# Sums of squares with fewer one-column matmuls, and reciprocal row sums brought to 64 partitions through DRAM instead of by transposes

## The chip, the cores and the metric

The kernel runs on one core of one Trainium2 chip. The metric is the device time of one execution in microseconds; smaller is better. The core has five engines that run in parallel, each working off its own queue in order: TensorE (PE, with its weight loads as PEld), VectorE (DVE), ScalarE (ACT), GpSimd (POOL) and SyncE (SP). Here every DMA is issued from SP's queue. Matmuls and transposes write PSUM; DVE and ACT read PSUM and SBUF, POOL reads SBUF only.

## What is computed

Two layers of a decoder trunk on 1024 tokens of width 1024, in f32. The parts that matter here:

```
qa, ka, va -> y_a : window attention, 6 heads of 64
y_b : latent attention, causal, 6 heads of 64:
    p = softmax(scores);  y_b[q, h, :] = sum_k p[q, k] v[k, h, :]
y_c : gated chunks
y = concat(rms_norm(y_a, gw_a), rms_norm(y_b, gw_b), rms_norm(y_c, gw_c))
x = x + g1 * (y @ w_out)
... then a SwiGLU block, and after both layers a final rms_norm
```

`rms_norm` divides by the root of the mean of squares over a group's columns: 384 for y_a and for y_b. The softmax's division by the row sum is made after the product with v.

## The kernel before, in words

Tokens are cut into 8 tiles of 128 and into two halves of 512 (Q = 0, 1). Matmuls are made in three passes over a high and a low part of each operand (`mm3`, lines 134 to 136), so that most matrices are split by ACT (the high part) and DVE (the low part, line 139).

Each layer has these stages. **Stage A**: input projections and window attention, with the latent projections. **Stage B**: latent attention, 12 groups (head, half), first the six heads of half 1 and then those of half 0. **Tail of B**: the output projection's tiles are mixed in with the last groups. Then normalisation, the SwiGLU block in two large stages, all matmul.

Within a stage the work is a set of generators, and a string written out by hand (`PRU0`, `PRU1` for A; `PRB0`, `PRB1` for B) says which takes its next step. A scheduler then puts each engine's instructions in a fixed order at compile time, near the program's, where an instruction that is not ready may be passed by a later one.

**y_a (stage A).** `a_av` writes a tile's window-attention output in transposed form, 3 chunks of 128 columns, for 128 tokens. ACT squares it (line 940). `group_rstd` sums the squares over the 384 columns with matmuls whose moving operand is one column of ones: three for a tile, added up in PSUM (line 540). DVE copies the sums out (542), and POOL's `rstd` makes the power -1/2 (171, 172). An f32 matmul is two passes in the trace.

**y_b (stage B).** Per group: `head_prep` transposes q and k; `b_soft` makes scores and exponentials of 4 tiles with their row sums in `sm`, [128, 4]; `b_av` has two generators. `gen_t` takes the reciprocals of `sm` (line 1197) and transposes the probabilities to `pTs`, unit by unit. `gen_m` multiplies with v, and its end `fin` makes the output: four transposes (line 1221) bring the reciprocals, broadcast along 64 columns, to 64 partitions in a PSUM bank `rT`; ACT and DVE add the two halves of the product (1223, 1225), and DVE multiplies by `rT` into `y32` (1226). After every two heads of a half `sq_pair` squares the 128x512 chunk (ACT, line 949), sums it with four one-column matmuls (953), copies the four columns out (955) and adds them to the last sum on POOL (957); after the third it calls `rstd`.

**The output projection.** `w_out`'s columns 0 to 511 were prepared earlier and are loaded as `wo`. Columns 512 to 1023 are loaded in `load_wout` as eight 128x512 tiles `wor` (line 1239), multiplied on POOL by the gate row `mrow` (line 1090), and split by ACT (146) and DVE (147) into `woh` and `wol`. `out_tile` uses them for the tiles of its second column half. `load_x` (1252) loads residual tiles as buffers of the tag "g" come free.

**Buffers.** A tag has a fixed number of buffers. "ad" has 4 of 128x512 f32 (`AD`): `qk` and `lowk` in stage A, `wor` in the tail of B, others later. "s" has 4 (`SM`): `sqB`, `tmpB` and more. PSUM in B has 4 single banks (`PA`: `pTB`, `qkTB`, `avB`, `rT`, `sq`) and 2 double ones (`PB`: scores).

Of the kernel before, what the change touches and what calls it, by code (L numbers as in the profile page):

```python
# [8 lines left out]
F32 = mybir.dt.float32  # L9
F32R = mybir.dt.float32r  # L10
I32 = mybir.dt.int32
AF = mybir.ActivationFunctionType
ALU = mybir.AluOpType
AX = mybir.AxisListType

P = 128
# [4 lines left out]
DEPTH = 2  # L21
# [57 lines left out]
def tile_trunk(ctx, tc, x, c, positions, ada_w, ada_b, norm1_w, w_in, a_sinks, b_q_norm_w, b_w_uq,  # L79
# [3 lines left out]
    ACT, DVE, POOL, PE, DMA = nc.scalar, nc.vector, nc.gpsimd, nc.tensor, nc.sync  # L83
# [5 lines left out]
    dr = ctx.enter_context(tc.tile_pool(name="dr", bufs=1, space=bass.MemoryType.DRAM))  # L89
    uid = [0]  # L90

    def nm(s):
        uid[0] += 1
        return f"{s}_{uid[0]}"
# [13 lines left out]
    def G(shape, dt=F32, name="g"):  # L108
        return gp.tile(shape, dt, tag="g", name=nm(name), bufs=NG)
# [7 lines left out]
    def SM(shape, dt=F32, name="s"):  # L117
        return sp.tile(shape, dt, tag="s", name=nm(name))

    def TN(w=8, name="t"):  # L120
        t = tp.tile([P, 8], F32, tag="t", name=nm(name))
        return t[:, :w]

    def PA(name="pa"):
        return ps_pool["a"].tile([P, 512], F32, tag="a", name=nm(name))
# [23 lines left out]
    def AD(name="ad", shape=(P, 512), dt=F32):  # L149
        return sp.tile(list(shape), dt, tag="ad", name=nm(name), bufs=NAD)  # L150

    def chunk(ap, k):
        return ap[:, k * P:(k + 1) * P]

    psum_banks(8, 0)
    ident = cst.tile([P, P], F32, name="ident")
    make_identity(nc, ident)
    ones = cst.tile([P, P], F32, name="ones")
# [10 lines left out]
    def rstd(dst, ss, n, w=1):  # L169
        v = TN(w, "ms")  # L170
        POOL.tensor_scalar(out=v, in0=ss, scalar1=1.0 / n, scalar2=EPS, op0=ALU.mult, op1=ALU.add)  # L171
        POOL.tensor_tensor(out=dst, in0=v, in1=mhalf[:, :w], op=ALU.pow)  # L172
# [180 lines left out]
    def rope(q, nh, half, t, f0):  # L353
# [20 lines left out]
    wpd = [{j: [dr.tile([P, 2, 512], F32, name=f"wp{l}_{j}_{i}") for i in range(7)] for j in EARLY[l]}  # L374
           for l in range(DEPTH)]
    cqd = [[dr.tile([P, 384], F32, name=f"cq{l}_{t}") for t in range(NT)] for l in range(DEPTH)]
    yad = [[dr.tile([P, 3, 512], F32, name=f"ya{l}_{hf}") for hf in range(2)] for l in range(DEPTH)]

    def ada_finish(l, j, mc, wait=1):
# [155 lines left out]
    def group_rstd(sq, n, dst):  # L535

        ps = PA("sq")
        for i in range(n):
            for k in range(3):
                PE.matmul(ps[:, i:i + 1], sq(k, i), ones[:, 0:1], start=(k == 0), stop=(k == 2))  # L540
        r = TN(n, "sc")
        DVE.tensor_copy(out=r, in_=ps[:, :n])
        rstd(dst, r, 384, n)

    def layer(l, x_tiles):
# [6 lines left out]
        rs_a = cst.tile([P, 8], F32, name=f"rsa{l}")  # L552
        rs_b = cst.tile([P, 8], F32, name=f"rsb{l}")
# [57 lines left out]
        y32 = [[None, None] for _ in range(4)]  # L611
# [38 lines left out]
        if l == 0:  # L650
# [39 lines left out]
            def l_seq():  # L690
                for kp in range(4):
                    if kp >= 2:
                        need("a", 8)
                    raw_w.append(load_w1(kp, acc0[0]))
                    yield

            def s_seq():
                for kp in range(4):
                    need("l", kp + 1)
                    split_w1(raw_w[kp], POOL if SP0[kp] else DVE)  # L700
                    yield

            def h_seq():
                need("s", 2)
                for t in range(NE):
                    need("m", t + 1)
                    avq[t] = PA("avq")
                    in_proj(avq[t], T[t], w1, 0, 4)
                    yield
# [30 lines left out]
            def g_seq():  # L740
# [6 lines left out]
                                    l=l_seq(), s=s_seq(), h=h_seq(), v=v_seq(), C=c_seq(), G=g_seq(), B=bg_seq()))  # L747
# [6 lines left out]
        else:  # L754
# [4 lines left out]
            for i, t in enumerate(ordA):  # L759
# [6 lines left out]
                ps = PA("avq")  # L766
# [19 lines left out]
        qk, qs_t, ks_t, qva, kwin, prs_a, y_a = {}, {}, {}, {}, {}, {}, {}  # L786
# [132 lines left out]
        def a_av(t, g):  # L919
            ph, pl = prs_a.pop((t, g))  # L920
            js = (1,) if t == 0 else (0, 1)
            po = PA("avA")
            for j in js:
                v = qva[t - 1 + j][:, 6 + g, :]
                PE.matmul(po[:, :384], v, ph[:, j, :], start=(j == js[0]), stop=False)
                PE.matmul(po[:, :384], v, pl[:, j, :], start=False, stop=(j == 1))
            tmp = SM([64, 384], F32, "tmpA")
            ACT.copy(out=tmp, in_=po[64:128, :384])
            if g == 0:
                y_a[t] = G([P, 2, 3, P], F32, "yA")  # L930
            for i in range(3):
                h = 3 * g + i
                k, r0 = h // 2, (h % 2) * 64
                DVE.tensor_tensor(out=y_a[t][r0:r0 + 64, 0, k, :], in0=chunk(po[0:64, :], i), in1=chunk(tmp, i),
                                  op=ALU.add)
            if g == 1:
                y = y_a.pop(t)
                hf, tt = t // 4, t % 4
                DMA.dma_start(out=yad[l][hf][:, :, tt * P:(tt + 1) * P], in_=y[:, 0])
                ACT.activation(out=y[:, 1], in_=y[:, 0], func=AF.Square)  # L940
                return lambda: group_rstd(lambda k, i: y[:, 1, k, :], 1, rs_a[:, t:t + 1])

        sqs = {}

        def sq_pair(p, Q):

            k = 3 + p
            sq = SM([P, 512], F32, "sqB")
            ACT.activation(out=sq, in_=y32[k // 2][Q][:, k % 2, :], func=AF.Square)
            yield  # L950
            ps = PA("sq")
            for i in range(4):
                PE.matmul(ps[:, i:i + 1], chunk(sq, i), ones[:, 0:1], start=True, stop=True)
            r = sqs[p, Q] = TN(4, "sc")
            DVE.tensor_copy(out=r, in_=ps[:, :4])
            if p > 0:
                POOL.tensor_tensor(out=r, in0=r, in1=sqs[p - 1, Q], op=ALU.add)
            if p == 2:
                rstd(rs_b[:, 4 * Q:4 * Q + 4], r, 384, 4)

# [210 lines left out]
        def b_av(h, Q, prs, sm):  # L1173

            d = 4 * Q
            units = [(j,) for j in range(d + 1)] + [(d + 1, d + 3), (d + 2,)]

            def tr(u):
                pt_ = PA("pTB")
                o = max(0, u[0] - d) * P if len(u) == 1 else 0  # L1180
                spans = []
                for j in u:
                    a = max(0, j - d)
                    s0 = 0 if j != u[0] else a * P
                    for i in range(a, 4):
                        c = s0 + (i - a) * P
                        PE.transpose(pt_[:, c:c + P], prs[i][:, j * P:(j + 1) * P], ident)
                    spans.append((j, a * P, slice(s0, s0 + (4 - a) * P)))
                pt2 = R([P, 2, 512], F32R, "pTs")
                ACT.copy(out=pt2[:, 0, o:], in_=pt_[:, o:])  # L1190
                sub(DVE, pt2[:, 1, o:], pt_[:, o:], f32(pt2[:, 0, o:]))
                return spans, pt2

            ready = []

            def gen_t():
                DVE.reciprocal(out=sm, in_=sm)
                for u in units:
                    ready.append(tr(u))
                    yield  # L1200

            def gen_m():
                po = PA("avB")
                for n in range(len(units)):
                    if n >= len(ready):
                        step("T")
                    spans, pt2 = ready[n]
                    last = n + 1 == len(units)
                    for j, o, cs in spans:
                        v = vB[j][:, h].rearrange("p a e -> p (a e)")  # L1210
                        PE.matmul(po[:, o:], v, pt2[:, 0, cs], start=(n == 0), stop=False)
                        PE.matmul(po[:, o:], v, pt2[:, 1, cs], start=False, stop=last)
                    yield
                fin(po)
                done.append(h)
                yield

            def fin(po):
                pr_ = PA("rT")
                for i in range(4):  # L1220
                    PE.transpose(pr_[:64, i * P:(i + 1) * P], sm[:, i:i + 1].to_broadcast([P, 64]), ident)
                tmp = SM([64, 512], F32, "tmpB")
                ACT.copy(out=tmp, in_=po[64:128, :])
                k, r0 = 3 + h // 2, (h % 2) * 64
                DVE.tensor_tensor(out=tmp, in0=po[0:64, :], in1=tmp, op=ALU.add)
                DVE.tensor_tensor(out=y32[k // 2][Q][r0:r0 + 64, k % 2, :], in0=pr_[:64, :], in1=tmp, op=ALU.mult)

            return gen_t(), gen_m()

# [381 lines left out]
        ready = []  # L1611
# [74 lines left out]
        def pair_seq():  # L1686
# [5 lines left out]
                    t=build_t_seq(), j=load_gu_seq(), r=prep_gu_seq(), s=pair_seq())  # L1692
# [71 lines left out]
```

## Time and profile before

| | |
|---|---|
| time, median of 3 runs | 2386.37 us (2384.11 to 2387.43) |
| the profiled execution | 2389.68 us, span 2387.7 us |
| mean granted TensorE clock | 0.979 |
| PE busy, share of the span | 2261.8 us, 95% |
| DVE | 1792.9 us, 75% |
| ACT | 1100.3 us, 46% |
| POOL | 1024.3 us, 43% |
| DMA, mean over the span | 146 GB/s |

How to read the profile: busy time is the time in which an engine has an instruction under way. Matmuls overlap, since the next starts while the last drains, so the time that one holds PE is read from the start of one to the start of the next. A group row gives the count, then the busy time in us and the mean in ns of one instruction, then the idle time of its engine just before it and what ended that. Rows in order of time give start and length in us. A wait row gives who waited for whom: total us, times, longest. Stage A is at about 130 to 330 us in layer 0 and 1300 to 1500 in layer 1, B with its tail at 339 to 469 and 1526 to 1656.

### The profile page before, as it was taken

To read this page: it belongs to the slowest core of one execution; us is meant where nothing else is said; L and a number is where in the kernel's file an instruction comes from. 1 tells how busy PE (TensorE), PEld (TensorE's weight loads), DVE (VectorE), ACT (ScalarE), POOL (GpSimd) and SP (SyncE) were. 2 spreads that over 40 slices of the span, in tenths; PEclk is the share of its full clock that TensorE was granted. 3 is DMA by queue.
4 is the path that set the end of the run, shared out by engine and by line. 5 is a ranking of instruction groups with operands and counts; after the bars stand their busy time and mean duration, and the time that the engine had idled before them with its cause. 6 is when DMAs were issued, how large, how long until landed. Compare 5 with 4: busy or idle time off the path is not lost. (4 is left out here: it accounts for less than half of the span.)

```text
span 2387.7 us, 31998 instructions
## 1 busy us (share of the span) xinstructions
PE 2261.8 (95%) x11195; PEld 1906.9 (80%) x11195; DVE 1792.9 (75%) x2787; ACT 1100.3 (46%) x2244; POOL 1024.3 (43%) x1011
## 2 busy tenths in 40 slices
PE   5999899998999999999999989899989999999998
PEld 4789798887887788778878878788877888887786
DVE  7787578859787776699974765788598767648978
ACT  4566377625333444223344654685354444433233
POOL 4755630343332433545554656212435334225643
PEclk9999999999999999999999999999999999999999
DMA  7403432312577654862241044323125545467433
GB/s 254 164 19 117 166 130 89 115 45 93 177 248 241 211 188 160 316 234 90 80 156 40 24 130 168 111 80 115 54 77 192 194 153 182 164 217 286 158 106 115
DMA packets 156036, 349.77 MB, mean 146 GB/s; under 512 B 12618, under 2 KB 71780, under 8 KB 155876
## 3 DMA queue, kind: packets, MB, share of 16 engines
q1 hardware_dynamic: 155876, 347.74, 42.3%
q8 instruction: 88, 1.44, 0.3%
q14 instruction: 72, 0.59, 0.1%
HBM read 252.75 MB, written 94.94 MB: 146 GB/s over the span
## 5 line engine op out<-in xcount | busy, mean ns | idle before, releaser
L139 DVE TENSOR_TENSOR gus<-gur,gus 128x512 fp32r<-128x512 f32 x264 | 255.5, 985 | 59.9 <-ACT gus L142 59.0
L142 ACT CAST gus<-gur 128x512 fp32r<-128x512 f32 x264 | 160.9, 621 | 219.2 <-PE gate L136 85.0
L134 PE MATMUL down<-dnt,dns 128*128 128x512 f32 x616 | 241.8, 393 | 13.2 <-ACT dnt L142 6.8
L134 PE MATMUL gate<-hTh,gus 128*128 128x512 f32 x616 | 242.8, 394 | 11.8 <-ACT u L1505 10.4
L135 PE MATMUL gate<-hTl,gus 128*128 128x512 f32 x616 | 241.4, 392 | 4.4 <-DVE hTl L139 4.4
L134 PE MATMUL up<-hTh,gus 128*128 128x512 f32 x616 | 241.0, 391 | 1.5 <-ACT u L1510 1.5
L135 PE MATMUL down<-dnt,dns 128*128 128x512 f32 x616 | 241.2, 391 | 0.0
L136 PE MATMUL down<-dnt,dns 128*128 128x512 f32 x616 | 240.8, 391 | 0.0
L136 PE MATMUL gate<-hTh,gus 128*128 128x512 f32 x616 | 240.8, 391 | 0.0
L135 PE MATMUL up<-hTl,gus 128*128 128x512 f32 x616 | 240.6, 391 | 0.0
L136 PE MATMUL up<-hTh,gus 128*128 128x512 f32 x616 | 240.4, 390 | 0.0
L1417 POOL TENSOR_TENSOR gur<-gur 128x512 f32<-128x512 f32 x44 | 67.2, 1528 | 389.6 <-DVE gus L139 389.6
L142 ACT CAST dns<-act 128x512 fp32r<-128x512 f32 x132 | 81.8, 622 | 250.3 <-PE down L136 189.6
L1595 DVE TENSOR_TENSOR x<-x,down 128x512 f32<-128x512 f32 x224 | 148.1, 679 | 31.5 <-PE down L136 31.2
L134 PEld LDWEIGHTS down<-dnt,dns 128*128 128x128 f32 x616 | 116.4, 189 | 41.2 <-issue 6.0
L134 PEld LDWEIGHTS gate<-hTh,gus 128*128 128x128 f32 x616 | 116.4, 189 | 39.1 <-ACT u L1505 12.3
L139 DVE TENSOR_TENSOR dns<-act,dns 128x512 fp32r<-128x512 f32 x132 | 136.3, 1048 | 12.9 <-ACT dns L142 12.9
L135 PEld LDWEIGHTS gate<-hTl,gus 128*128 128x128 f32 x616 | 116.4, 189 | 29.5 <-DVE hTl L139 6.0
L134 PEld LDWEIGHTS up<-hTh,gus 128*128 128x128 f32 x616 | 116.4, 189 | 26.1 <-ACT u L1510 2.0
L136 PEld LDWEIGHTS down<-dnt,dns 128*128 128x128 f32 x616 | 116.5, 189 | 24.3
L136 PEld LDWEIGHTS gate<-hTh,gus 128*128 128x128 f32 x616 | 116.4, 189 | 24.4
L135 PEld LDWEIGHTS up<-hTl,gus 128*128 128x128 f32 x616 | 116.3, 189 | 24.1
(410 smaller groups left out, 6165.1 us busy)
## 6 DMA issues: line engine op xcount, KB each, us to landing
gur<-in_w_gate_up_dram SPq DMA_DIRECT2D x88, 512.0 KB
ada<-in_ada_w_dram SPq DMA_DIRECT2D x80, 512.0 KB
wp<-wpe SPq DMA_DIRECT2D x77, 512.0 KB
dnt<-wp SPq DMA_DIRECT2D x77, 512.0 KB
dnr<-in_w_down_dram SPq DMA_DIRECT2D x44, 512.0 KB
act<-act SPq DMA_DIRECT2D x44, 512.0 KB
wr<-in_w_in_dram SPq DMA_DIRECT2D x24, 512.0 KB
act<-u SPq DMA_DIRECT2D x44, 256.0 KB
```

Source lines behind the costliest of these rows:

```text
L134: PE.matmul(ps, lh, rh, start=start, stop=False, skip_group_check=more)
L135: PE.matmul(ps, lh, rl, start=False, stop=False, skip_group_check=more)
L136: PE.matmul(ps, ll, rh, start=False, stop=stop, skip_group_check=more)
L139: eng.tensor_tensor(out=out_, in0=a, in1=b, op=ALU.subtract)
L142: ACT.copy(out=h, in_=src)
L1417: return lambda o, a, b, op: eng.tensor_tensor(out=o, in0=a, in1=b, op=op)
L1595: DVE.tensor_tensor(out=av_, in0=av_, in1=ps[t], op=ALU.add)
```

## The change

Four edits.

1. `a_av` squares into chunks 3 to 5 of one tile, and POOL adds the second and third chunk's squares to the first's (two 128x128 adds for each of 16 tiles). `group_rstd` takes the sum, so there is one one-column matmul for a tile instead of three.
2. `sq_pair` keeps the first pair's squares in an `AD` buffer; DVE adds the second's and third's squares to it (128x512), and the one-column matmuls are made once for a half, in `group_rstd`, instead of after every two heads. The three copies and two small POOL adds become one copy.
3. `gen_t` stores the reciprocals right after they are made: `sm`, [128, 4], goes to a DRAM tile of 4 rows of 128, in pieces of one element; a second DMA loads the 512 values as one row onto each of 64 partitions, into an `AD` buffer `rB`.
4. `fin` multiplies by `rB` instead of `rT`; the four transposes and their PSUM bank go.

```diff
+    rsd = [[[dr.tile([4, P], F32, name=f"rs{l}_{h}_{hf}") for hf in range(2)] for h in range(6)] for l in range(DEPTH)]
...
         for i in range(n):
-            for k in range(3):
-                PE.matmul(ps[:, i:i + 1], sq(k, i), ones[:, 0:1], start=(k == 0), stop=(k == 2))
+            PE.matmul(ps[:, i:i + 1], chunk(sq, i), ones[:, 0:1], start=True, stop=True)
...
-                DMA.dma_start(out=yad[l][hf][:, :, tt * P:(tt + 1) * P], in_=y[:, 0])
-                ACT.activation(out=y[:, 1], in_=y[:, 0], func=AF.Square)
-                return lambda: group_rstd(lambda k, i: y[:, 1, k, :], 1, rs_a[:, t:t + 1])
+                DMA.dma_start(out=yad[l][hf][:, :, tt * P:(tt + 1) * P], in_=y[:, 0:3])
+                ACT.activation(out=y[:, 3:6], in_=y[:, 0:3], func=AF.Square)
+                for k in (4, 5):
+                    POOL.tensor_tensor(out=y[:, 3, :], in0=y[:, 3, :], in1=y[:, k, :], op=ALU.add)
+                return lambda: group_rstd(y[:, 3, :], 1, rs_a[:, t:t + 1])
...
-            sq = SM([P, 512], F32, "sqB")
+            sq = AD("sqB") if p == 0 else SM([P, 512], F32, "sqB")
             ACT.activation(out=sq, in_=y32[k // 2][Q][:, k % 2, :], func=AF.Square)
             yield
-            ps = PA("sq")
-            for i in range(4):
-                PE.matmul(ps[:, i:i + 1], chunk(sq, i), ones[:, 0:1], start=True, stop=True)
-            r = sqs[p, Q] = TN(4, "sc")
-            DVE.tensor_copy(out=r, in_=ps[:, :4])
-            if p > 0:
-                POOL.tensor_tensor(out=r, in0=r, in1=sqs[p - 1, Q], op=ALU.add)
+            if p == 0:
+                sqs[Q] = sq
+            else:
+                DVE.tensor_tensor(out=sqs[Q], in0=sqs[Q], in1=sq, op=ALU.add)
             if p == 2:
-                rstd(rs_b[:, 4 * Q:4 * Q + 4], r, 384, 4)
+                group_rstd(sqs[Q], 4, rs_b[:, 4 * Q:4 * Q + 4])
...
-            ready = []
+            ready, rb = [], []
 
             def gen_t():
                 DVE.reciprocal(out=sm, in_=sm)
+                DMA.dma_start(out=rsd[l][h][Q].rearrange("i p -> p i"), in_=sm)
+                rb.append(AD("rB", [64, 512]))
+                DMA.dma_start(out=rb[0], in_=rsd[l][h][Q].rearrange("i p -> (i p)").partition_broadcast(64))
...
             def fin(po):
-                pr_ = PA("rT")
-                for i in range(4):
-                    PE.transpose(pr_[:64, i * P:(i + 1) * P], sm[:, i:i + 1].to_broadcast([P, 64]), ident)
...
-                DVE.tensor_tensor(out=y32[k // 2][Q][r0:r0 + 64, k % 2, :], in0=pr_[:64, :], in1=tmp, op=ALU.mult)
+                DVE.tensor_tensor(out=y32[k // 2][Q][r0:r0 + 64, k % 2, :], in0=rb[0], in1=tmp, op=ALU.mult)
```

More of the change, by code (lines that the diff above doesn't have):

```diff
@@ L929, in a_av @@
             if g == 0:
-                y_a[t] = G([P, 2, 3, P], F32, "yA")
+                y_a[t] = G([P, 7, P], F32, "yA")
             for i in range(3):
@@ L933, in a_av @@
                 k, r0 = h // 2, (h % 2) * 64
-                DVE.tensor_tensor(out=y_a[t][r0:r0 + 64, 0, k, :], in0=chunk(po[0:64, :], i), in1=chunk(tmp, i),
+                DVE.tensor_tensor(out=y_a[t][r0:r0 + 64, k, :], in0=chunk(po[0:64, :], i), in1=chunk(tmp, i),
                                   op=ALU.add)
```

## The prediction

> **What bounds the kernel now.** I read the page's busy table first, then a table by stage, then PE and DVE in order of time around the lines that the change touches, then SP's waits. The page:
>
> ```profile
> PE 2261.8 (95%) x11195; PEld 1906.9 (80%) x11195; DVE 1792.9 (75%) x2787; ACT 1100.3 (46%) x2244; POOL 1024.3 (43%) x1011
> ```
>
> PE is busy 95% on average. What a PE instruction is worth depends on the stage. By stage (start:end, length, then PE, PEld, DVE, ACT, POOL busy, granted clock, DMA share, GB/s):
>
> ```profile
> 130.00:330.00 200.00, 186.99 (x1175) 171.98 (x1173) 142.63 (x347) 112.41 (x298) 126.08 (x198) 0.97 0.35 116
> 339.00:438.00 99.00, 98.65 (x641) 85.39 (x641) 85.22 (x179) 77.33 (x164) 9.71 (x7) 1.00 0.20 66
> 438.00:469.00 31.00, 31.00 (x179) 26.68 (x178) 29.44 (x57) 20.06 (x42) 11.30 (x9) 1.00 0.56 186
> 1300.00:1500.00 200.00, 184.89 (x1120) 167.00 (x1119) 134.39 (x343) 108.83 (x291) 119.96 (x188) 0.96 0.33 105
> 1526.00:1625.00 99.00, 98.68 (x643) 85.52 (x642) 85.30 (x181) 77.56 (x165) 9.71 (x7) 1.00 0.19 67
> 1625.00:1656.00 31.00, 31.00 (x179) 26.65 (x179) 29.54 (x57) 20.35 (x42) 10.86 (x8) 1.00 0.57 182
> ```
>
> Rows one and four are stage A of the two layers (projections, window attention), where PE idles 13.0 and 15.1 us of 200. Rows two and five are the latent attention (call it B): PE idles 0.3 us of 99, DVE is busy 86%, ACT 78%, and the clock is full. PE time taken out there shortens the run until DVE binds. Rows three and six are B's tail, where output tiles mix with the last heads: PE is full, but DVE is busy 95% too, so PE time is worth little there.
>
> **The change, part by part: what PE loses.** PE in order of time (start, length, line; the L1221 row is one head's four transposes, the L953 row one `sq_pair`'s four f32 matmuls, two passes each; L540 is one tile of y_A):
>
> ```profile
> 458.78 0.60 PE L1221 MATMUL rT<-ident,smB 128*64 128x128 f32 x4
> 459.13 0.48 PE L134 MATMUL oC<-wo,yTh 128*128 128x512 f32 x1
> 459.45 0.39 PE L135 MATMUL oC<-wo,yTh 128*128 128x512 f32 x1
> 459.68 0.40 PE L136 MATMUL oC<-wo,yTl 128*128 128x512 f32 x1
> ...
> 463.78 0.95 PE L953 MATMUL sq<-ones,sqB 128*128 128x1 f32 x8
> 464.59 0.49 PE L134 MATMUL oAB<-wo,yTh 128*128 128x512 f32 x1
> 464.92 0.40 PE L135 MATMUL oAB<-wo,yTh 128*128 128x512 f32 x1
> ...
> 188.66 0.73 PE L540 MATMUL sq<-ones,yA 128*128 128x1 f32 x6
> 189.25 0.74 PE L914 MATMUL pTA<-ident,pA 128*128 128x128 f32 x5
> ```
>
> Durations overlap, so I take starts. A 512-column matmul in a run steps 0.23 us (459.45 to 459.68). From 458.78 to 459.45 stand four transposes and one such matmul, 0.67 us, so a head's transposes hold PE 0.44 us; 12 heads-by-halves in each of two layers make 24 x 0.44 = 10.6 us. From 463.78 to 464.92 is 1.14 us, less 0.23 is 0.91 us for one `sq_pair`; 12 become 4, so 8 x 0.91 = 7.3 us. Six passes of y_A hold 0.59 us and four of the six go: 0.39 x 16 tiles = 6.3 us. Gross 24.2 us: 17.9 in B, half of it per layer (8.9), and 6.3 in A. In B the nine heads and two `sq_pair`s ahead of the tail make 9 x 0.44 + 2 x 0.91 = 5.8 us per layer; the tail holds the other 3.1.
>
> **What DVE and POOL get.** The rows (count | busy, mean ns):
>
> ```profile
> L1226 DVE TENSOR_TENSOR y32b<-rT,tmpB 64x512 f32<-64x512 f32 x16 | 10.9, 679 | 0.3
> L139 DVE TENSOR_TENSOR yTl<-y32b,yTh 128x1024 fp32r<-128x1024 f32 x2 | 2.4, 1216 | 0.0
> L139 DVE TENSOR_TENSOR yTl<-y32ab,yTh 128x1024 fp32r<-128x1024 f32 x2 | 3.7, 1827 | 0.0
> L955 DVE COPY sc<-sq 128x4 f32<-128x4 f32 x12 | 1.9, 160 | 2.6 <-PE sq L953 2.6
> L362 POOL TENSOR_TENSOR QK<-r,r 128x96 f32<-128x96 f32 x16 | 8.6, 540 | 0.0
> L362 POOL TENSOR_TENSOR qk<-r,r 128x256 f32<-128x256 f32 x16 | 13.0, 813 | 0.0
> ```
>
> `sqB` adds: no row has 128x512 with both inputs in SBUF in B; half of the 128x1024 rows gives 0.61 to 0.91 us, and I take 0.61, since POOL is almost idle there. Two adds per half less two copies of 0.16: +0.9 us per half, +1.8 per layer. The final multiply reads `rB` in SBUF instead of PSUM: 0.61 for 0.68, 12 x 0.07 = 0.8 us less per layer. DVE in B before the tail stays near 86 us against 99 - 5.8 = 93: 92%. PE remains the bound, barely. I count three quarters of 5.8 as real: 4.4 us per layer, 8.7 in all; ends 0 and 5.8. The four fewer one-bank PSUM allocations (`rT`, `sq`) can only loosen the queue and are counted at nothing. POOL loses 8 tiny adds (L957) of slack work.
>
> y_A's two adds are 128x128, between 0.54 (96 columns) and 0.81 us (256): I take 0.6, 32 x 0.6 = 19 us of POOL, in a stage where POOL is busy 60 to 63%. They sit between ACT's square and the PE pass, so the pass becomes ready 1.2 us later, plus what stands ahead on POOL. PE idles there for other reasons already, so I count 0.6 of the 6.3 us: 3.8; ends -3 and 6.3.
>
> **The transfer chain.** Reciprocals go out in 512 pieces of 4 bytes and come back on 64 partitions. Nearest rows: a 4 KB store that a load waited for, and a broadcast on 128 partitions that POOL waited for; then reciprocal and final multiply of the first head (339.12, 352.88), of a middle one and of the last.
>
> ```profile
> 654.78 0.30 SPq L391 DMA_DIRECT2D mod<-mr  x1
> 656.06 0.35 SPq L466 DMA_DIRECT2D mrow<-mod  x1
> ...
> 1514.73 0.32 SPq L466 DMA_DIRECT2D mrow<-mod  x1
> 1519.36 5.06 POOL L1090 TENSOR_TENSOR wor<-wor,mrow 128x512 f32<-128x512 f32 x4 [14.04 <-DMA mrow<-mod]
> ...
> 339.12 0.16 DVE L1197 RECIPROCAL smB<-smB 128x4 f32<-128x4 f32 x1
> 352.88 0.67 DVE L1226 TENSOR_TENSOR y32ab<-rT,tmpB 64x512 f32<-64x512 f32 x1
> 420.21 0.16 DVE L1197 RECIPROCAL smB<-smB 128x4 f32<-128x4 f32 x1
> 428.12 0.68 DVE L1226 TENSOR_TENSOR y32ab<-rT,tmpB 64x512 f32<-64x512 f32 x1
> 455.62 0.18 DVE L1197 RECIPROCAL smB<-smB 128x4 f32<-128x4 f32 x1
> 461.46 0.69 DVE L1226 TENSOR_TENSOR y32b<-rT,tmpB 64x512 f32<-64x512 f32 x1
> ```
>
> Store to load: 1.3 us (654.78 to 656.06). Broadcast: 4.6 us (1514.73 to 1519.36) for 512 KB, an upper end for 128 KB. Together 5.9 at most if 512 small pieces cost what 8 long rows do; I allow 1 us more for them. Cover: 13.8, 7.9 and 5.8 us. So it is hidden but for the last head of each layer, up to 1.1 us; I count 0.5 each. If that cover goes, DVE stands in its queue at the multiply, and with it the `pTs` subtractions that PE's next matmuls read. In all 48 DMAs enter SP's queue, whose loads of x, wo and w_out wait behind the 1.3 us of each store.
>
> **AD buffers and w_out.** `rB` (12 per layer) and the long-lived `sqB` now use the four AD buffers that the `wor` loads use:
>
> ```profile
> 312.95 0.33 SPq L1239 DMA_DIRECT2D wor<-in_w_out_dram  x1
> 332.59 5.07 POOL L1090 TENSOR_TENSOR wor<-wor,mrow 128x512 f32<-128x512 f32 x4 [5.11 <-DMA mrow<-mod]
> ...
> 468.81 0.39 PE L134 MATMUL oC<-woh,yTh 128*128 128x512 f32 x1
> ```
>
> Today four of the eight are loaded by 325 and gated on idle POOL at 333. Their place in the program is behind the eleventh `rB`, so with buffers handed out in program order they load only from about 438, and all eight gates (1.27 us each, the row's quarter) fall in the tail, before PE asks for them at 469. Per buffer: load 2.8 (443.49 to 446.31 below), gate 1.27, split 0.7 + 0.75: 5.5 us. Three buffers free, eight tiles: three rounds, 16.5 us, done near 455 to 470. I count 1 us of PE waiting in each tail, ends 0 and 8, and no gain there from the 3.1 us.
>
> ```profile
> 443.49 5.15 SPq L1239 DMA_DIRECT2D wor<-in_w_out_dram  x2
> 446.31 1.30 POOL L1090 TENSOR_TENSOR wor<-wor,mrow 128x512 f32<-128x512 f32 x1 [18.08 <-DMA wor<-in_w_out_dram]
> 442.67 0.75 DVE L147 SCALAR_TENSOR_TENSOR wol<-wor,cols,woh 128x512 fp32r<-128x512 f32 x1
> 438.19 0.72 ACT L146 ACTIVATE woh<-wor,cols 128x512 fp32r<-128x512 f32 x1
> ```
>
> **Sum.** 8.7 (B) + 3.8 (A) - 1 (last heads) - 2 (tails) = 9.5; what the freed PSUM banks give makes me round up to 11. The profiled execution took 2389.7 us (span 2387.7, 2.0 around it), 3.3 above the median 2386.4. It would become 2378.7; on the scale of the median I predict 2375.5.
>
> **Rivals.** (1) All of it counts: PE stays the bound in A and in the tail, 24.2 us, 2362. For it: the tail's PE has no idle microsecond. Against: DVE at 95% there.
>
> (2) DVE and POOL take it back, no change. The 1827 ns row against 1216 for the same shape is DVE working while POOL does: 0.6 us lost per meeting. Four more gates per tail and 32 POOL adds in A, each meeting one DVE instruction: 8 + 32 = 40 x 0.6 = 24 us of DVE at most, and where half of it lands on the path, 12 us: 2386.4 - 11 + 12 = 2387. It decides if DVE passes PE in A, where it is at 67 to 71%; that speaks against. The Trainium skill (SBUF — State Buffer, "Who interferes with whom") makes it harsher: a DVE instruction with two SBUF inputs and a GpSimd one that reads SBUF exclude each other for a whole instruction. By that rule the multiply, moved from PSUM to SBUF, joins the exposed ones; the trace agrees in kind (1827 against 1216).
>
> (3) Slower: a store caught in SP's queue. SP is in order, and x loads wait in it for a buffer:
>
> ```profile
> SPq L1252 <- PE qkTB L1151: 23.8, 1, 23.8
> ```
>
> A store queued behind such a load leaves up to 23.8 us late, against 13 us of cover, and DVE and then PE stand for up to 10 us. With two such places per layer at 6 us each, 24 us: 2386.4 - 11 + 24 = 2399. It decides from 5.5 us per layer on. For it: the queue's order is fixed at compile time by estimated times. Against: both events follow PE's own progress, so their order is easily got right. The skill (DMA: Bandwidth & Descriptors, "Specifications") says that pieces below 512 B are read, changed and written back; no run here has stores of 4 bytes.
>
> (4) The change does nothing at all: excluded in B, where PE has no idle time to absorb it, unless (2).
>
> **Chances.** Forecast 0.50 (its own range 2368 to 2381); (1) 0.15; (2) 0.19; (3) 0.16. A measurement tells 0.2%, 4.8 us: faster below 2381.6. Faster 0.65, same 0.19, slower 0.16. The range leaves out (3) and little else: 2361 to 2390.
>
> **What would show it.** PE busy in B falls by about 9 us per layer and the stage by 4 to 5; L1221 is gone, L953 and L540 fall from 96 passes each to 32 in `group_rstd` for each. DVE busy in B rises by about 1 us per layer and its idle time names no `rB` load except at the last head. POOL in A is up 8 to 11 us per layer. `wor` loads start near 430 rather than 313. I am wrong if DVE waits for `rB` at many heads (3), if DVE's two-SBUF rows lengthen (2), or if PE waits for `woh` for more than a few us.

## The result, and the profile after

The changed kernel takes 2530.4 us (median of 4 runs, 2526.5 to 2542.1) against 2385.2 us (4 runs, 2384.0 to 2387.4): a ratio of 1.0605, interval [1.0587, 1.0623], or 145 us slower. Forecast were 2375.5 us in a range of 2361 to 2390: the sign was wrong, and the time lies far outside the range. The profiled execution took 2533.0 us (span 2531.0).

The busy table of the changed kernel's page:

```profile
PE 2283.8 (90%) x10971; PEld 1914.9 (76%) x10971; DVE 1805.6 (71%) x2787; ACT 1102.4 (44%) x2244; POOL 1035.6 (41%) x1035
```

PE runs 224 matmuls fewer, as many as the edits take away, and is busy 22 us *longer*. The table by stretch says where (columns as in the prediction's table; B and its tail in layer 0, cut in two; first two rows before, last two after):

```profile
340.00:420.00 80.00, 79.79 (x525) 69.38 (x525) 69.52 (x142) 62.82 (x130) 4.92 (x5) 1.00 0.22 73
420.00:530.00 110.00, 108.63 (x566) 91.26 (x565) 75.66 (x129) 45.92 (x103) 38.10 (x32) 1.00 0.24 82
340.00:420.00 80.00, 67.81 (x411) 57.89 (x409) 58.00 (x114) 53.20 (x107) 0.00 (x0) 0.94 0.10 21
420.00:530.00 110.00, 69.09 (x309) 56.69 (x310) 51.35 (x114) 40.64 (x93) 12.64 (x9) 0.74 0.48 98
```

PE, which idled 0.2 and 1.4 us there before, now idles 12 us of the first 80 and 41 us of the next 110, and the granted clock falls to 0.74, so that what is left of its work also takes longer. The waits name two places, DVE at the final multiply (first two rows, whole span) and SP at the load of `rB` (layer 0's B, layer 1's B):

```profile
DVE y32b L1225 <- DMA rB<-rs: 47.6, 11, 9.2
DVE y32ab L1225 <- DMA rB<-rs: 38.0, 7, 8.2
...
SPq L1199 <- DMA rs<-smB: 103.1, 10, 12.2
...
SPq L1199 <- DMA rs<-smB: 106.7, 11, 11.5
```

In order of time, the first head: reciprocal, store, load, the multiply that stood for the load, and PE behind it.

```profile
341.80 0.16 DVE L1196 RECIPROCAL smB<-smB 128x4 f32<-128x4 f32 x1
...
341.99 0.37 SPq L1197 DMA_DIRECT2D rs<-smB  x1
351.38 0.51 SPq L1199 DMA_DIRECT2D rB<-rs  x1
...
362.47 0.68 DVE L1225 TENSOR_TENSOR y32ab<-rB,tmpB 64x512 f32<-64x512 f32 x1 [6.81 <-DMA rB<-rs]
...
363.81 1.11 PE L1186 MATMUL pTB<-ident,pB 128*128 128x128 f32 x4 [6.84 <-DVE kTl L139]
```

From store to load pass 9.4 us here and 8.8 to 13.3 us over all 24 (10.8 in the middle), not 1.3. And SP stands in the meantime with the other loads behind it. The `w_out` loads, at 313 and 443 us before, now begin at 502, and what they feed stands in every engine's order ahead of the last head:

```profile
502.13 1.05 SPq L1238 DMA_DIRECT2D wor<-in_w_out_dram  x2
...
507.76 2.48 POOL L1089 TENSOR_TENSOR wor<-wor,mrow 128x512 f32<-128x512 f32 x2 [47.29 <-DMA wor<-in_w_out_dram]
...
509.06 0.72 ACT L146 ACTIVATE woh<-wor,cols 128x512 fp32r<-128x512 f32 x1 [9.21 <-POOL wor L1089]
...
511.76 1.12 PE L1186 MATMUL pTB<-ident,pB 128*128 128x128 f32 x4 [6.34 <-ACT pB L1170]
```

### The profile page after: what moved, and what is told of

Read it like the earlier page. It is cut to its first block, busy times and chain, and to the rows that moved or that the text cites. A ratio compares the mean times of both kernels' runs of the same rounds, so it can differ in the third digit from the quotient of the medians.

```text
span 2531.0 us, 31649 instructions
## 1 busy us (share of the span) xinstructions
PE 2283.8 (90%) x10971; PEld 1914.9 (76%) x10971; DVE 1805.6 (71%) x2787; ACT 1102.4 (44%) x2244; POOL 1035.6 (41%) x1035
## 5 line engine op out<-in xcount | busy, mean ns | idle before, releaser
L1594 DVE TENSOR_TENSOR x<-x,down 128x512 f32<-128x512 f32 x224 | 147.8, 678 | 30.3 <-PE down L136 29.9
L134 PEld LDWEIGHTS down<-dnt,dns 128*128 128x128 f32 x616 | 116.4, 189 | 41.9 <-issue 6.0
L134 PEld LDWEIGHTS up<-hTh,gus 128*128 128x128 f32 x616 | 116.8, 190 | 26.3 <-ACT u L1509 2.0
L136 PEld LDWEIGHTS gate<-hTh,gus 128*128 128x128 f32 x616 | 117.0, 190 | 24.8
L136 PEld LDWEIGHTS up<-hTh,gus 128*128 128x128 f32 x616 | 116.4, 189 | 24.6
```

The lines of the kernel that those rows point to most:

```text
L134: PE.matmul(ps, lh, rh, start=start, stop=False, skip_group_check=more)
L136: PE.matmul(ps, ll, rh, start=False, stop=stop, skip_group_check=more)
L1594: DVE.tensor_tensor(out=av_, in0=av_, in1=ps[t], op=ALU.add)
```

## The experiments

The table gives stage lengths of each run's profile, read from start times: "A" from the first window-attention reciprocal (`smA`) to the first latent one (`smB`), "heads" from the first to the last `smB` reciprocal, "tail" from there to the last matmul on `wo` or `woh`, "FF" (feed-forward; one expectation calls it the mixture stages) from there to the last `gate` matmul, the sum of both layers. Two values are layer 0 and layer 1. Times are medians; runs with a ratio were timed beside the kernel before, the others have one time, that of the profiled execution.

| run | A | heads | tail | FF | us | ratio |
|---|---|---|---|---|---|---|
| before | 212.4, 231.1 | 116.5, 116.4 | 86.9, 86.9 | 875.7 | 2385.2 | |
| before again | 212.3, 228.4 | 116.5, 116.5 | 86.9, 86.9 | 875.3 | 2385.6 | |
| after | 215.8, 223.7 | 169.9, 165.2 | 106.1, 107.8 | 880.6 | 2530.4 | 1.0605 [1.0587, 1.0623] |
| e1 squares only | 215.7, 225.2 | 117.5, 117.4 | 88.1, 87.6 | 878.2 | 2393.5 | 1.0033 [1.0020, 1.0046] |
| e2 DRAM only | 213.3, 223.6 | 157.9, 154.9 | 102.2, 104.3 | 879.4 | 2495.4 | 1.0460 [1.0445, 1.0476] |
| e3 no store | 218.0, 224.1 | 113.1, 114.2 | 91.4, 91.6 | 878.0 | 2393.8 | 1.0034 [1.0021, 1.0048] |
| e4 rows of 512 B | 216.8, 226.2 | 124.8, 124.3 | 96.2, 96.5 | 879.4 | 2426.7 | 1.0170 [1.0153, 1.0187] |
| e5 chain unused | 216.1, 224.6 | 146.7, 147.8 | 104.6, 104.1 | 877.1 | 2482.6 | 1.0402 [1.0382, 1.0421] |
| e6 chain on POOL | 216.0, 224.2 | 165.5, 160.6 | 104.7, 104.9 | 879.8 | 2509.8 | 1.0511 [1.0470, 1.0553] |
| e8 pieces of 16 B | 215.9, 224.2 | 117.5, 116.4 | 97.7, 97.9 | 878.4 | 2411.9 | 1.0108 [1.0091, 1.0125] |
| e9 no chain | 214.3, 225.3 | 114.0, 115.1 | 87.1, 87.1 | 880.7 | 2387.0 | 0.9998 [0.9985, 1.0011] |
| e10 y_A only | 215.8, 230.0 | 117.0, 116.4 | 86.7, 87.0 | 876.5 | 2390.6 | 1.0023 [1.0013, 1.0033] |
| e11 `sq_pair` only | 211.9, 224.5 | 117.4, 117.5 | 88.4, 87.6 | 877.7 | 2386.8 | 1.0007 [0.9994, 1.0019] |
| e17 128 pieces of 4 B | 216.0, 224.4 | 160.1, 158.5 | 103.9, 104.0 | 880.6 | 2510.4 | |
| e18 free reciprocals | 212.2, 228.8 | 114.7, 114.5 | 87.2, 87.2 | 882.0 | 2388.0 | 1.0004 [0.9992, 1.0016] |
| e18 again | 213.6, 227.2 | 114.6, 114.7 | 87.2, 87.2 | 883.3 | 2389.8 | |
| e19 POOL, 16 B, own buffer | 212.1, 228.8 | 117.8, 118.9 | 97.8, 96.1 | 878.6 | 2411.7 | 1.0106 [1.0088, 1.0124] |
| e20 4 B, 64 B apart | 214.9, 223.9 | 127.6, 125.8 | 98.8, 100.0 | 882.8 | 2437.1 | |

**Which half loses.** e1 is the kernel before with edits 1 and 2, e2 with edits 3 and 4.

> Only the squares are added up ahead of the one-column matmuls; the reciprocals are transposed by PE as in the kernel before. Theory T (the 4-byte store lands 9 to 13 us after its issue and everything lost comes from that): no loss, and the gain of this part alone, 7.3 us in the latent attention and 6.3 in stage A at most, so 2370 to 2384 us, and no wait of DVE above its old ones. Rival S (the squares' adds on DVE and POOL, or the long-lived sqB in a buffer shared with the w_out loads, carry part of the loss): over 2395 us.

> Only the reciprocals go through DRAM; the squares are as in the kernel before. T: the whole loss stays, 2520 to 2545 us, with some 85 us of DVE waiting for rB. Rival S: under 2500 us.

The chain through DRAM alone makes 109 us, the squares 8; together they make 145, so some 28 us come from their meeting. e2's 2495.4 us is therefore its rival's case (under 2500), not the theory's: the squares carry part of the loss, but only 8 us of it without the chain. e1 falls between its two cases: no large loss, but no gain either.

**The store.** e3 takes the store away and leaves the load:

```diff
-DMA.dma_start(out=rsd[l][h][Q].rearrange("i p -> p i"), in_=sm)
-DMA.dma_start(out=rb[0], in_=rsd[l][h][Q].rearrange("i p -> (i p)").partition_broadcast(64))
+DMA.dma_start(out=rb[0], in_=norm2_w[l, 0:512].partition_broadcast(64))
```

> The changed kernel without the 512-piece store; the broadcast load into rB stays in its place and its buffer, but reads 512 numbers of norm2's weight row, which wait for nothing (left out: y_b is multiplied by those numbers, not by the reciprocals). T: the load is early at every head, DVE does not wait for it, 2362 to 2395 us. Rival B (rB in the buffers that the w_out loads use, or the 24 broadcast loads themselves, carry a large part): over 2430 us, with PE waiting for woh and wol at the end of each layer.

2393.8 us: of the 145 us, 137 go with the store. DVE never waits for `rB`. The other four change the shape of the store.

```diff
 e4: PE.transpose of sm to [4, 128], ACT.copy to s4, then
+DMA.dma_start(out=rsd[l][h][Q], in_=s4)                       # 4 rows of 512 B
 e8: rsd is [128, 4]
+DMA.dma_start(out=rsd[l][h][Q], in_=sm)                       # 128 pieces of 16 B
 e17:
+DMA.dma_start(out=rsd[l][h][Q][0:1, :].rearrange("i p -> p i"), in_=sm[:, 0:1])
 e20: rsd is [128, 16]
+DMA.dma_start(out=rsd[l][h][Q][:, 0:1], in_=sm[:, 0:1])       # each 64 B from the next
```

> The changed kernel with the store's layout changed on the chip first: one PE transpose of the 128x4 reciprocals to 4x128, one copy by ACT, and a store of 4 rows of 512 B in place of 512 pieces of 4 B. T in its narrow form (the pieces are slow, not the way through DRAM): store to load falls from 9.4-13 us to 1.3-2.5, plus about 1 us for transpose and copy, and the time to 2370 to 2400 us. Rival R (any store followed by a load of the same bytes costs what was seen, since the load waits for the completion of the store): store to load stays above 6 us and the time above 2470 us.

> The changed kernel with the store as 128 pieces of 16 bytes, one for each partition, and the broadcast load reading them as they lie (left out: the order of the 512 numbers, so y_b is multiplied by permuted reciprocals). From store to load 9.4-13 us were seen with 512 pieces of 4 B and 1.2 us with 4 pieces of 512 B. Theory N (time goes with the number of pieces): about 1.2 + (124/508) x 9 = 3.4 us, and 2400 to 2430 us. Rival P (any piece far below 512 B costs the whole delay): 8 us or more, and 2490 to 2530 us. Rival E (only single 4-byte elements are slow): under 1.6 us, and 2393 to 2400 us.

> The changed kernel with only the first column of reciprocals stored: 128 pieces of 4 B in place of 512 (loaded four times into rB; left out: three quarters of the reciprocals, so y_b is multiplied by wrong ones). 512 pieces of 4 B took 8.8 to 13.3 us from store to load, 128 of 16 B 1.4 (2.0 in the middle), 4 of 512 B 1.2. Theory N (the number of 4-byte pieces sets it): 1.2 + (124/508) x 9.6 = 3.5 us. Rival E (a 4-byte piece alone makes it slow, whatever the number): 8 us or more. Rival Z (small stores are cheap up to some number): 1.4 to 2 us. The time is only looked at: four loads for each head stand in SP's queue.

> As the run with 128 pieces of 4 B (6.7 to 12.0 us from store to load), but each piece 64 B from the next in DRAM rather than beside it; one load that gathers the 128 numbers (left out: three quarters of the reciprocals; the gathering load is itself slow, so the time is only looked at). Theory J (neighbouring 4-byte pieces hinder each other): store to load falls to 1.4-2 us. Rival E (a 4-byte piece is slow by itself): it stays at 6.5 us or more.

First store and load of layer 0 in each of the four, from their timelines of SP, in the order e4, e8, e17, e20:

```profile
344.79 0.26 SPq L1201 DMA_DIRECT2D rs<-s  x1
346.02 0.51 SPq L1203 DMA_DIRECT2D rB<-rs  x1
```

```profile
343.34 0.32 SPq L1197 DMA_DIRECT2D rs<-smB  x1
344.81 0.51 SPq L1199 DMA_DIRECT2D rB<-rs  x1
```

```profile
344.66 0.32 SPq L1197 DMA_DIRECT2D rs<-smB  x1
351.63 2.43 SPq L1200 DMA_DIRECT2D rB<-rs  x4
```

```profile
341.38 0.32 SPq L1197 DMA_DIRECT2D rs<-smB  x1
342.83 0.64 SPq L1199 DMA_DIRECT2D rB<-rs  x1
```

1.2, 1.5, 7.0 and 1.4 us; the middle ones of 24 are 1.2, 1.8, 8.2 and 1.5 (in e8 and e20 a few are longer, up to 5.5 and 4.9). e17 and e20 both store 128 numbers of 4 B; only the distance in DRAM differs. So what makes a store slow is 4-byte pieces side by side: 128 of them cost 8.2 us, 512 cost 10.8. As many pieces 64 B apart, or as many of 16 B, cost little. Distances between 4 and 64 B were not tried. e8's 1.8 us lies between its cases of 1.6 and 3.4; e17 refutes that the number of pieces alone sets the price (3.5 us). The Trainium skill (DMA: Bandwidth & Descriptors, "Specifications") says that pieces below 512 B are read, changed and written back; pieces of 16 B, or of 4 B set apart, take at most 0.6 us more here, in the middle, than e4's rows of 512 B. In the changed kernel the 512 pieces' packets ran at once:

```profile
DMA  0000640000000000000000000000000000000000
...
DMA packets 528, 0.00 MB, mean 0 GB/s; under 512 B 528, under 2 KB 528, under 8 KB 528
```

That is the window from 341.9 to 351.4 us in 40 slices of 0.24 us: packets in the fifth and sixth, then 8 us with none until the load. The time is between the last packet and the completion that the load waits for. What happens there no run shows; that neighbours must be merged into one stretch of memory one after another is a guess.

e4 and e8 have fast stores and still lose 41 and 24 us (e4 missed its 2370 to 2400 us). So some 118 of the 137 us that go with the store go with its slowness (after against e8), and 18 come with any store (e8 against e3). In e4 the new transpose and copy stand in PE's and ACT's order (heads +8 us); in both the tail is 9 to 11 us longer: SP stands at each *store* until DVE has made the reciprocals (90.6 us in e8's layer 0), and the loads of `w_out` come at 459 us and later (e4). That the late loads make the tails longer was not tested by itself.

**Direct wait or queue.** e5 issues both transfers as the changed kernel does, but multiplies by `rT`, transposed as before; e6 issues both from POOL's queue.

```diff
 e5:
+pr_ = PA("rT")
+for i in range(4):
+    PE.transpose(pr_[:64, i * P:(i + 1) * P], sm[:, i:i + 1].to_broadcast([P, 64]), ident)
-DVE.tensor_tensor(out=y32..., in0=rb[0], in1=tmp, op=ALU.mult)
+DVE.tensor_tensor(out=y32..., in0=pr_[:64, :], in1=tmp, op=ALU.mult)
 e6: both DMA.dma_start of gen_t become POOL.dma_start
```

> Both transfers are issued as in the changed kernel, in the same places of SP's queue and into the same buffers, but the final multiply takes the reciprocals from PE transposes as in the kernel before, so that DVE waits for no transfer. Theory D (the direct wait of DVE makes the loss): the 86 us of DVE waiting for rB go, and with them what follows; 2393 (the squares alone) plus up to 15: 2393 to 2410 us. Rival Q (SP's queue, in which x, wo and w_out wait behind each store, and the buffers make it): 2470 us or more, with PE and DVE waiting for wo, x and woh in the last part of each layer. Between: the share of each.

> Both transfers of the changed kernel are issued from POOL's queue and not from SP's; the 512 pieces and DVE's wait stay. Q: SP's loads are early again, PE waits for wo and x go, and the time falls to 2440-2490 us. D: the wait for rB is as long as before, the time stays within 25 us of the 2530 of the changed kernel, or is longer if POOL stands ahead of the store in its own order (POOL then also delays the gates of w_out).

I had held the direct wait to be the loss; e5 says otherwise. With no wait of DVE for `rB`, 95 us of the 145 remain. Its stretches, to be set against the changed kernel's two above:

```profile
340.00:420.00 80.00, 79.75 (x511) 68.72 (x512) 70.44 (x139) 63.99 (x131) 2.39 (x1) 1.00 0.12 29
420.00:530.00 110.00, 71.75 (x338) 58.26 (x337) 56.18 (x108) 39.65 (x83) 20.80 (x17) 0.78 0.55 136
```

Up to 420 us PE is full and 100 matmuls ahead of the changed kernel (24 are its own transposes of the reciprocals): what the changed kernel loses there is the direct wait's. From 420 on it is as empty as there, though nothing waits for `rB`. In order of time:

```profile
446.85 0.80 PE L134 MATMUL oAB<-wo,yTh 128*128 128x512 f32 x1 [5.66 <-DMA wo<-wo]
...
456.12 0.37 ACT L1189 CAST pTs<-pTB 128x256 fp32r<-128x256 f32 x1 [13.12 <-PE pTB L1186]
...
486.95 2.49 POOL L1089 TENSOR_TENSOR wor<-wor,mrow 128x512 f32<-128x512 f32 x2 [47.20 <-DMA wor<-in_w_out_dram]
488.24 0.72 ACT L146 ACTIVATE woh<-wor,cols 128x512 fp32r<-128x512 f32 x1 [10.16 <-POOL wor L1089]
...
490.95 1.11 PE L1186 MATMUL pTB<-ident,pB 128*128 128x128 f32 x4 [9.36 <-ACT pB L1170]
```

The loads of `wo` and `w_out` are late, output tiles and the splits of `w_out` stand before the last heads in PE's, ACT's and POOL's order, and the heads behind them stand too. In e6 SP no longer stands at the store, but DVE's wait stays, and POOL stands (73.6 us for the store in layer 0). A third thing shows there: the loads of `w_out` are still late, at 482 us, since SP waits there for loads of `rB` into the buffers that they share.

```profile
SPq L1238 <- DMA rB<-rs: 71.1, 3, 44.9
```

The loss is 122 us. So e5, with a blocked queue, late buffers and the squares' 8 us but no waiting multiply, keeps two thirds of the loss. e6 does not isolate DVE's wait, since POOL's standing and the buffers are in it; what that wait makes by itself stays open, and the shares overlap.

**The ideal.** e9 has no chain at all (the multiply reads a column of ones); e18 has that on the kernel before, without edits 1 and 2; e10 and e11 are edits 1 and 2 alone.

```diff
-DVE.tensor_tensor(out=y32..., in0=rb[0], in1=tmp, op=ALU.mult)
+DVE.tensor_tensor(out=y32..., in0=ones[:64, 0:1].to_broadcast([64, 512]), in1=tmp, op=ALU.mult)
```

> The changed kernel without any transfer and without rB: the final multiply reads a column of ones that is in SBUF all the time (left out: y_b is not multiplied by the reciprocals). This is what the change would bring if the way to the 64 partitions were free in time, queue and buffers. Theory F (the terms of the prediction for PE hold, and what the run with the free load lost was rB in the buffers of the w_out loads): the tail loses its 4.5 us per layer, and the time is 2372 to 2386 us. Rival G (PE's freed time is not worth anything, since DVE sets the pace and every row that is added on DVE costs): 2388 to 2396 us, as with the free load.

> The kernel before with the squares of y_A alone added up on POOL ahead of the one-column matmuls (stage A); latent attention and reciprocals as before. The squares of both places together measured 1.0033 [1.0020, 1.0046]. Theory A (this part costs, by POOL and the waits of stage A): 2390 to 2396 us, with the stretch before layer 0's latent attention 2 to 4 us longer. Rival A' (this part gains, and the part in the latent attention costs): 2376 to 2384 us, with layer 1's stage A 5 us or more shorter.

> The kernel before with the squares of y_b alone added up on DVE, the first of each three in one of the four buffers of the w_out loads; stage A and the reciprocals as before. Theory H (the adds on DVE cost what PE gains, since DVE is nearly full there): B and tail within +-1 us of before in each layer, 2385 to 2390 us. Rival L (the long-lived sqB pushes the w_out loads, and that costs): tails 1 us or more longer each, 2389 to 2395 us.

> The kernel before, squares untouched, without the transposes of the reciprocals and without any transfer in their place: the final multiply reads a column of ones (left out: y_b is not multiplied by the reciprocals). The bound of what the second half of the change can bring. Theory M (the prediction's own working: PE's 0.44 us for a head are real in the latent attention as long as DVE is not loaded further; the squares ate it in the run without any transfer): the latent attention 3 to 5 us shorter in each layer, tails as before, 2374 to 2381 us. Rival G (DVE sets the pace and PE's time is worth nothing): 2384 to 2389 us.

> The run with free reciprocals once more (left out again: y_b is not multiplied by the reciprocals), for one look at the stage lengths. In its first profile the latent attention was 1.8 us shorter in each layer, but the two mixture stages behind it, where nothing was changed, took 452.1 + 429.9 = 882.0 us against 875.7 and 875.3 in the two profiles of before, so that nothing was left. Theory K (what is freed comes back later, in the mixture stages, as a property of the kernel): 880 us or more again. Rival V (one execution's share of the granted clock): 875 to 878 us, and a total 3 to 5 us under before.

> The kernel before once more, as a measure of how far the lengths of stages differ between two executions of one kernel. Theory V (the 231.1 us of layer 1's stage A in the profile of before are one execution's share, since a kernel whose stage A is the same has 223.6): 223 to 229 us here. Rival W (it belongs to the kernel): 230 us or more.

Not even a free transfer makes the change pay: 2387.0 us, between what the theory and its rival expected. By parts: y_A costs 0.23% [0.13, 0.33]; layer 0's stage A is 3.4 us longer, though PE has less to do there (layer 1's, 230.0, lies between the two of before). `sq_pair` is worth nothing: PE loses 1.9 us of work in the heads of each layer, and the heads take some 1.0 us longer. The adds, in e11's trace (least, median and longest in ns), with 0.61 us assumed:

```profile
L954 DVE TENSOR_TENSOR sqB<-sqB,sqB x8: 674/688/1736, 398.4 to 1649.7; 128x512 f32<-128x512 f32 x8
```

Free reciprocals shorten the heads by 1.7 to 1.9 us in each layer, in both profiles, not by the 3 to 5 expected; PE loses 4.0 and 4.2 us of work there, and the other half is not on the path. The median shows nothing of the 3.7 us of both layers; in the two profiles FF takes 882.0 and 883.3 us instead of 875.7 and 875.3, which is more than was gained. The first layer's FF in before (first row) and e18:

```profile
542.57:990.21 447.64, 428.92 (x1894) 352.26 (x1893) 336.76 (x402) 184.38 (x326) 153.65 (x99) 0.98 0.58 198
```

```profile
539.86:991.93 452.07, 431.51 (x1894) 353.90 (x1893) 339.97 (x402) 184.30 (x326) 152.57 (x99) 0.98 0.58 196
```

The same 1894 matmuls hold PE 2.6 us longer, and its idle time grows by 1.8. The surplus does not sit still: the first profile of e18 has 4.4 us of it in layer 0, the second 5.6 us in layer 1 (433.7 against 428.1). All sixteen profiles of other kernels have a longer FF (876.5 to 883.3) than both of before. Why is open. Layer 1's stage A of 231.1 us came out at 228.4 in before again, inside the bounds of the theory that it was one execution's share; but the other kernels speak for a share of the kernel's own. It is 224 to 226 in the kernels that put `rB` or `sqB` into the buffers of `w_out`, and 227 to 231 in those that don't, as if the `w_out` work that leaves stage A were the difference; that was not tested by itself.

**A repair.** e19 takes the three causes away: 16-byte pieces, POOL's queue, an own buffer whose lower half serves even heads and whose upper half odd ones; squares as before (to make room, a pool of small tiles and the tile of ones shrink).

```diff
+POOL.dma_start(out=rsd[l][h][Q], in_=sm)
+POOL.dma_start(out=rbt[q0:q0 + 64, :], in_=rsd[l][h][Q].rearrange("p i -> (p i)").partition_broadcast(64))
+DVE.tensor_tensor(out=..., in0=rbt[q0:q0 + 64, :].rearrange("q (p i) -> q i p", i=4), in1=..., op=ALU.mult)
```

> The kernel before, squares untouched, with the reciprocals through DRAM in another way: 128 pieces of 16 B (1.4 us from store to load, uncontended) in place of 512 of 4 B; both transfers on POOL's queue, so that SP's loads of x, wo and w_out do not stand behind them; one fixed 2 KB buffer for rB, even heads in its lower and odd heads in its upper 64 partitions, so that the w_out loads keep their four buffers; the multiply reads rB with a step of 16 B. If the three causes found so far (4-byte pieces, SP's queue, the shared buffers) are all: within 4 us of the run with free reciprocals, and 2375 to 2386 us. If a cause is left (POOL's own order, a step of 16 B on DVE, the broadcast load of some 4 us against a cover of 5.8 to 13.8): 2390 us or more, and the profile names it by DVE's waits at the multiply or by the multiply's own duration.

It comes out at 2411.7 us: causes are left, and the tails are 10.8 and 9.1 us longer. The multiply that reads `rB` with a step of 16 B takes 1.08 us, not 0.68 (12 x 0.4 = 4.8 us of DVE for each layer), and the last head's load is late, with POOL's order between store and load:

```profile
L1228 DVE TENSOR_TENSOR y32b<-rB,tmpB x16: 1056/1080/1093, 376.5 to 1668.0; 64x512 f32<-64x512 f32 x16
```

```profile
DVE y32b L1228 <- DMA rB<-rs: 6.1, 1, 6.1
```

Since the free run gains nothing over before (0.9992 to 1.0016), a better way through DRAM has nothing to gain either, unless what FF takes back can be had. No kernel here is faster than the one before by more than the noise.

## Why the prediction was wrong, point by point

**The store's price: the step that failed.** 1.3 us came from a store of eight long rows, and 1 us was added for 512 small pieces. Measured: 10.8 us. The row was the nearest in kind (a store that a load waits for), but nothing in the trace bounded small neighbouring pieces from above, and the text took its own estimate for an end. Hence "hidden but for the last head", against a cover of 13.8, 7.9 and 5.8 us, became 85.6 us of DVE waiting in 18 places.

**What stands behind the wait.** The prediction wrote that SP's loads "wait behind the 1.3 us of each store", and saw in its third rival a store caught behind a load. It went the other way: the loads of x, `wo` and `w_out` were caught behind the *load* that waits for the store. e5 shows 95 us with this and the squares' 8, and no wait of DVE. The cost of a blocked queue was not bounded by the store's price but by what is queued.

**PE's gain in B** (4.4 us a layer counted, ends 0 and 5.8). Without any transfer the heads are 2.5 and 1.3 us shorter (e9), from the transposes (e18: 1.8). The squares give back what they take (e11). The adds take 0.69 us, one of eight 1.74, and not 0.61, on a DVE that is 87% busy in the heads; that this is why was not tested. The transposes' own price was nearly right: PE loses 4.0 and 4.2 us of work, and ten heads' transposes lie in that stage, 4.4 us at 0.44 each. Counting three quarters was too much: somewhat under half holds for the transposes, nothing for the squares.

**y_A** (3.8 us counted, ends -3 and 6.3). A loss of 0.23% [0.13, 0.33], 3 to 8 us in all, past the lower end. The adds were sized right (0.6 us; in the changed kernel's groups 609 ns); the sign was not.

```profile
L942 POOL TENSOR_TENSOR yA<-yA 128x128 f32<-128x128 f32 x32 | 19.5, 609 | 8.9 <-ACT yA L940 8.0
```

The prediction feared the adds in the chain from the square to the sums. In layer 0's stage A of e10, PE waits 0.2 us at the sums, yet idles 17.8 us against 13.0, at other places (before, then e10):

```profile
PE qT L870 <- DVE nmA L897: 2.8, 1, 2.8
PE lowT L803 <- DMA cqr<-cq: 1.2, 1, 1.2
...
PE qT L869 <- DVE nmA L896: 3.8, 1, 3.8
PE lowT L802 <- DMA cqr<-cq: 2.7, 1, 2.7
PE qT L869 <- DVE yA L933: 1.2, 1, 1.2
PE sq L539 <- DVE smA L901: 0.2, 1, 0.2
```

DVE, which gets nothing new there, is 2 us busier, most of it in twelve subtractions that the edit leaves alone (before, then e10):

```profile
L139 DVE TENSOR_TENSOR ks<-qk,ks 128x128 fp32r<-128x128 f32 x12 | 4.1, 378 | 0.0
L139 DVE TENSOR_TENSOR ks<-qk,ks 128x128 fp32r<-128x128 f32 x12 | 5.7, 511 | 0.0
```

e1, which has the same edit, shows both again. This is what rival 2 foresaw in kind, DVE slower beside a busier POOL; no run separates it from the mere shift in time.

**AD buffers** (1 us a tail, ends 0 and 8). The mechanism was right and the size within its bounds: with a free load into `rB` (e3) the tails are 4.5 and 4.6 us longer, without `rB` (e9) 0.2. The multiply gained nothing: 0.68 us, not 0.61.

**The sum.** Its terms made 9.5 us and were rounded up to 11 for PSUM banks that the working had counted at nothing; no run shows that term, and e9 gains nothing.

**The rivals.** That all 24 us count is refuted by e9. Contention of DVE and POOL (rival 2) is not what made 145 us, but its signs are in stage A, and the 2387 us that it gave are e9's, the kernel without transfers; that the numbers meet is no proof. The third rival named the right queue and the right sign, but the wrong victim: it priced a store caught behind a load of x, 12 us a layer from one wait of 23.8 us, and in the changed kernel SP waits 0.2 us in all at its loads of x.

**The clock.** The prediction took no account of it. Where PE stands, its granted clock falls, to 0.74 between 420 and 530 us. Layer 0's heads, before and after:

```profile
339.12:455.62 116.50, 116.15 (x747) 100.48 (x745) 101.64 (x216) 90.35 (x194) 15.59 (x11) 1.00 0.21 70
```

```profile
341.80:511.74 169.94, 124.02 (x669) 103.84 (x667) 101.21 (x213) 88.53 (x191) 10.82 (x7) 0.84 0.31 62
```

78 matmuls fewer hold PE 8 us longer. The Trainium skill (TensorE: Matmul & The Clock Gate, "What's actually happening") says that the gate falls to half rate after an idle window of about 3.4 us; the trace agrees, in that the mean is 1.00 in e5's full stretch and 0.78 in its empty one, and that the changed kernel's 512-column matmuls step by 0.43 us behind a wait, against 0.23 in a run at full clock. How long an idle time it takes no run here shows.

```profile
499.70 0.63 PE L136 MATMUL oAB<-wo,yTl 128*128 128x512 f32 x1
500.13 0.63 PE L134 MATMUL oAB<-wo,yTh 128*128 128x512 f32 x1
```

## What to carry to other kernels

Price a DMA by a row of the same shape, pieces and neighbours included; where there is none, measure it first, for here a store of 2 KB took 10.8 us to the load behind it and one of 4 KB 1.3. A load that waits for a store in an in-order queue costs what stands behind it in that queue, so list that first; here 95 of 145 us stayed though nobody used what was loaded (e5). Ask also which buffers a slow transfer keeps from others. And with one engine 99% busy and another at 87% beside it, somewhat under half of what was taken off the first was gained here, and nothing where the second got work for it.

## What was not expected of the hardware

A store of 128 numbers of 4 B takes 8.2 us from issue to the load that waits for it when they lie side by side in DRAM, and 1.5 us when they lie 64 B apart; side by side in pieces of 16 B it takes 1.8. In the first store of the changed kernel and of e17, the packets are over within 1.4 us of the issue. A DVE multiply of 64x512 with one operand at a step of 16 B took 1.08 us against 0.68.
